# All experts' rows added to the residual on TensorE by one-hot products, gate and up in blocks of 32 slots, and another order of the experts

## The chip, the cores and the metric

One NeuronCore of a Trainium2 chip runs the whole kernel in one launch. The metric is the device time of one execution in microseconds; the median of three runs counts. The engines named below are PE (TensorE, matrix products and transposes), PEld (its weight loads, which go beside the products), DVE (VectorE), ACT (ScalarE), POOL (GpSimd) and SP (SyncE, which here issues the big DMAs).

## What is computed

Two transformer blocks over 512 tokens of width 1024, all in float32. The second block ends in a mixture of 32 experts, and only that part is touched by the change. Cut to what matters:

```python
def hier_moe(h, w_rg, b_rg, w_re, b_re, w_gate, w_up, w_down):
    # every token picks one group, and two experts in it, with weights top_w
    ...
    # expert e, for the rows x of the tokens that chose it:
    y = (silu(x @ w_gate[e]) * (x @ w_up[e])) @ w_down[e]
    # each row is scaled by its weight and added to its token
    ...

x = x + hier_moe(rmsnorm_2(x, norm2_g), ...)
```

`w_gate[e]` and `w_up[e]` are 1024 x 512, `w_down[e]` is 512 x 1024: 6 MB an expert, 192 MB in all. 512 tokens with two experts each make 1024 rows. For the given inputs the rows of experts 0 to 31 are 37, 57, 10, 30, 27, 23, 34, 20, 37, 16, 26, 2, 21, 11, 16, 15, 26, 40, 42, 48, 11, 31, 11, 31, 48, 36, 10, 81, 25, 85, 78, 39. Thirteen experts have over 32 rows, three of them (27, 29, 30) over 64.

## The kernel before

Everything up to the router takes about 1,140 us and is the same in both kernels, but for one small thing named below. Then the experts run one after the other, in the order 31, 30, ... 0.

**Weights.** `fetch` issues them from SP's queue in units of 2 MB, each two DMAs of 1 MB: two units of an expert hold halves of gate and up together, and one holds down. A ring of 9 units (three experts) is filled ahead; from then on a unit is fetched when PE has done with the one in its place, and SP's queue takes them in the order of a list, `plan`: the two gate/up units of expert i, then the down unit of expert i - 1.

**Rows.** An expert's rows sit in slots, 64 to a block. POOL gathers a block with an indirect DMA. A row of 1024 is kept as two halves in partitions 0 to 63 and 64 to 127 (`xs`; `xb` for a second block).

**PE's work for one expert** is: two transposes of the activations of the expert before (`at`), four of the next expert's rows (`xt`), gate and up (`gu_half`, once for each half), and down of the expert before (`expert_down`, name `yy`). The array's 128 columns are used as two tiles of 64 columns, side by side: one tile for the output columns of c = 0 and one for c = 1. A float32 product of 512 columns stands in the trace as two PE instructions, so that a half of gate/up and a whole down are each 16 instructions.

**More than 64 rows.** `tc.If(cnt > SLOTS)` runs a second block of 64 slots (`gv`, then `yv` after the down). There are two such branches per expert; all engines have them.

**The way back.** `expert_y` scales the rows of `yy` by their weights on ACT, and POOL scatters them by an indirect DMA to a buffer in DRAM, `y_d`, where each token has two places. (`clear_y` has set that buffer to zero in the first block's MLP.) When all is scattered, `add_y` reads `y_d` back, 4 MB, and adds it to the residual `x2` on DVE and POOL. The last two experts (DIRECT = 2) don't go that way: `add_direct` multiplies a one-hot matrix (which slot belongs to which token, `owned`) by their rows on PE, 64 slots of a half in each half of the array's rows, and DVE adds the product to `x2`.

Of the kernel before, what the change touches and what calls it, by code (L numbers as in the profile page):

```python
# [9 lines left out]
F32 = mybir.dt.float32  # L10
# [10 lines left out]
P = 128  # L21
# [67 lines left out]
def tile_kernel(tc, I, out, dbg=None, stop=None):  # L89
# [1135 lines left out]
    DIRECT = 2  # L1225
# [74 lines left out]
    loads = []  # L1300

    def fetch(srcs):
# [5 lines left out]
        for i, src in enumerate(srcs):  # L1308
            loads.append(nc.sync.dma_start(raw[:, i * 2048:(i + 1) * 2048], src))
# [6 lines left out]
    def src_d(e):  # L1316
        return [wd_d[e].rearrange("(h p j) d -> h p (j d)", h=2, j=2)[h] for h in range(2)]


    seq = list(range(NE))[::-1]  # L1320
    plan = []
    for i in range(NE + 1):
        if i < NE:
            plan += [src_gu(seq[i], 0), src_gu(seq[i], 1)]
        if i:
            plan.append(src_d(seq[i - 1]))
# [137 lines left out]
    gi_, si_, wsl, tkf = [], [], [], []  # L1464
    tps_ = bank("t")
    for blk in range(2):
# [9 lines left out]
        tkf.append(tki)  # L1476
        si_.append(by_halves(f"si{blk}", orf)[0])
        wsl.append(slot_weights(rtp, tps_[:, (2 + blk) * NE:(3 + blk) * NE], oh, f"m{blk}"))
    tail_.__exit__(None, None, None)
# [11 lines left out]
    y_h = y_d.rearrange("s (h d) -> (s h) d", h=2)  # L1491
# [7 lines left out]
    def scatter(ys, idx, dst=y_h):  # L1499
# [17 lines left out]
    def gu_half(ps, xT, W, h):  # L1517
# [8 lines left out]
    def expert_act(ps, blk=""):  # L1526
        a_ = mp.tile([P, 256], F32, tag=f"act{blk}", bufs=1 if blk else 2, name=f"act{blk}{uid()}")
        nc.scalar.activation(a_, ps[:, 0:256], AF.Silu)  # L1528
        nc.vector.tensor_tensor(a_, a_, ps[:, 256:512], op=ALU.mult)  # L1529
        return a_  # L1530

    def expert_aT(a_, blk=""):
        tp = tr_bank("at")
        av = a_.rearrange("s (p j) -> s j p", j=2)
        for j in range(2):
            nc.tensor.transpose(tp[:, j * P:(j + 1) * P], av[:, j, :], ident)
        aT = mp.tile([P, 2, P], F32, tag=f"aT{blk}", bufs=1 if blk else 2, name=f"aT{blk}{uid()}")
        nc.scalar.activation(aT.rearrange("p j s -> p (j s)"), tp[:, 0:256], AF.Copy)  # L1538
        return aT
# [220 lines left out]
```

## Time and profile before

| | |
|---|---|
| median of three runs | 1661.91 us (1661.04 to 1663.17) |
| the profiled execution | 1661.64 us, its span 1659.9 us |
| PE busy | 1529.6 us, 92% of the span |
| PEld busy | 1059.6 us, 64% |
| DVE busy | 710.4 us, 43% |
| ACT busy | 532.3 us, 32% |
| POOL busy | 184.7 us, 11% |
| SP's DMA queue | 317.12 MB, 51.2% of the span of 16 engines |

The span is the stretch that the profiler recorded, and the device time is 1.74 us longer. The shares are means over stages that are bound by different things: the experts are the last 520 us, in which DVE has little to do.

### The profile page before, as it was taken

What the parts mean: (1) busy time and instruction counts of PE and PEld (TensorE: products, weight loads), DVE (VectorE), ACT (ScalarE), POOL (GpSimd) and SP (SyncE); (2) the same over time, 40 slices, a digit from 0 to 9 for tenths busy, and PEclk for the clock granted to TensorE, in tenths of its full rate; (3) what the DMA queues carried; (4) which work ended last, traced back from release to release, by engine and by line L of the source; (5) the groups of instructions that cost most, each with busy time, mean ns of one, the idle gap of its engine ahead of it and who ended that gap; (6) DMA issues with size and microseconds to landing.
All of it is one profiled execution on the core that took longest, in us unless ns stands there. A gap on an engine that the chain in (4) does not pass through costs nothing. (4 is left out here: it accounts for less than half of the span.)

```text
span 1659.9 us, 20583 instructions
## 1 busy us (share of the span) xinstructions
PE 1529.6 (92%) x7494; PEld 1059.6 (64%) x7494; DVE 710.4 (43%) x1562; ACT 532.3 (32%) x1033; POOL 184.7 (11%) x199
## 2 busy tenths in 40 slices
PE   7999999899999999899999999987999988788776
PEld 7887776688888888688888777774333333233332
DVE  7699636663335444646874545543000100000003
ACT  6444437643324343443455433220111110010010
POOL 1000001220000000140000000012122221211112
PEclk9999999999999999999999999997999999999998
DMA  5313105025233323234222326646899999999995
GB/s 174 115 52 94 38 22 178 26 66 202 89 101 115 103 88 102 90 115 130 77 66 70 121 96 241 212 173 266 351 374 410 414 415 417 416 416 416 417 418 241
DMA packets 99327, 328.90 MB, mean 198 GB/s; under 512 B 17474, under 2 KB 26258, under 8 KB 74114
## 3 DMA queue, kind: packets, MB, share of 16 engines
q1 hardware_dynamic: 90866, 317.12, 51.2%
q0 software_dynamic: 8336, 10.14, 1.7%
q8 instruction: 75, 1.23, 0.3%
q14 instruction: 50, 0.41, 0.1%
HBM read 321.27 MB, written 24.92 MB: 209 GB/s over the span
## 5 line engine op out<-in xcount | busy, mean ns | idle before, releaser
L127 PE MATMUL mm<-wh,Ah 128*128 128x512 f32 (+3 forms) x800 | 307.4, 384 | 6.6 <-DVE gate L1211 2.1
L1522 PE MATMUL gu<-mr,xT 128*64 128x512 f32 x1024 | 251.6, 630 | 55.8 <-DMA mr<-in_w_expert_up_dram 51.3
L128 PE MATMUL mm<-wl,Ah 128*128 128x512 f32 (+3 forms) x800 | 299.1, 374 | 0.7 <-DVE wl L134 0.7
L129 PE MATMUL mm<-wh,Al 128*128 128x512 f32 (+3 forms) x800 | 299.5, 375 | 0.0
L134 DVE TENSOR_TENSOR wl<-raw,wh 128x1024 fp32r<-128x1024 f32 (+3 forms) x160 | 185.0, 1163 | 117.6 <-ACT wh L133 114.3
L133 ACT ACTIVATE wh<-raw 128x1024 fp32r<-128x1024 f32 (+3 forms) x164 | 164.1, 1008 | 146.0 <-PE mm L128 117.4
L1522 PEld LDWEIGHTS gu<-mr,xT 128*64 128x64 f32 x1024 | 81.8, 144 | 201.9 <-issue 198.8
L127 PEld LDWEIGHTS mm<-wh,Ah 128*128 128x128 f32 x800 | 152.3, 190 | 33.3 <-issue 4.9
L127 PE MATMUL mm<-Ah,wh 128*128 128x512 f32 x416 | 169.4, 407 | 0.0
L129 PEld LDWEIGHTS mm<-wh,Al 128*128 128x128 f32 x800 | 151.9, 190 | 25.8 <-DVE Al L134 0.7
L128 PEld LDWEIGHTS mm<-wl,Ah 128*128 128x128 f32 x800 | 152.5, 191 | 23.8 <-DVE wl L134 1.2
L129 PE MATMUL mm<-Ah,wl 128*128 128x512 f32 x416 | 163.2, 392 | 0.0
L128 PE MATMUL mm<-Al,wh 128*128 128x512 f32 x416 | 163.2, 392 | 0.0
L253 POOL TENSOR_TENSOR rr<-rm,mhalf 128x1 f32<-128x1 f32 (+3 forms) x40 | 32.5, 815 | 991.4 <-DVE rm L252 991.3
L1529 DVE TENSOR_TENSOR act<-act,gu 128x256 f32<-128x256 f32 x32 | 13.5, 421 | 281.6 <-ACT act L1528 281.6
L1546 PE MATMUL yy<-mr,aT 128*64 128x512 f32 x512 | 117.3, 594 | 1.7 <-ACT aT L1538 0.9
L1528 ACT ACTIVATE act<-gu 128x256 f32<-128x256 f32 x32 | 12.3, 384 | 274.3 <-PE gu L1522 274.3
L128 PEld LDWEIGHTS mm<-Al,wh 128*128 128x128 f32 x416 | 78.3, 188 | 17.6 <-issue 2.9
L127 PEld LDWEIGHTS mm<-Ah,wh 128*128 128x128 f32 x416 | 78.3, 188 | 17.2 <-issue 2.9
L129 PEld LDWEIGHTS mm<-Ah,wl 128*128 128x128 f32 x416 | 78.3, 188 | 15.9
L1546 PEld LDWEIGHTS yy<-mr,aT 128*64 128x64 f32 x512 | 40.9, 137 | 70.8 <-issue 56.9
L1514 DVE COPY xT<-xt 128x512 f32<-128x512 f32 x35 | 24.2, 691 | 143.3 <-PE xt L1512 143.3
(379 smaller groups left out, 1921.6 us busy)
## 6 DMA issues: line engine op xcount, KB each, us to landing
mr<-in_w_expert_gate_dram SPq DMA_DIRECT2D x64, 1024.0 KB
mr<-in_w_expert_up_dram SPq DMA_DIRECT2D x64, 1024.0 KB
mr<-in_w_expert_down_dram SPq DMA_DIRECT2D x64, 1024.0 KB
raw<-in_w_in_dram SPq DMA_DIRECT2D x56, 512.0 KB
raw<-in_w_up_dram SPq DMA_DIRECT2D x32, 512.0 KB
raw<-in_w_down_dram SPq DMA_DIRECT2D x32, 512.0 KB
raw<-in_w_out_dram SPq DMA_DIRECT2D x16, 512.0 KB
y_d<-zero SPq DMA_DIRECT2D x4, 1024.0 KB
```

The source lines that it names most:

```text
L127: nc.tensor.matmul(ps, ah, bh, start=first, stop=False)
L128: nc.tensor.matmul(ps, ah, bl, start=False, stop=False)
L129: nc.tensor.matmul(ps, al, bh, start=False, stop=last)
L133: nc.scalar.activation(hi, src, AF.Copy)
L134: return lo_eng.tensor_tensor(lo, src, hi.bitcast(F32), op=ALU.subtract)
L253: nc.gpsimd.tensor_tensor(r[:, :n], m[:, :n], mhalf[:, :n], op=ALU.pow)
L1514: nc.vector.tensor_copy(xT.rearrange("p j s -> p (j s)"), tp)
L1522: nc.tensor.matmul(ps[c * 64:(c + 1) * 64, :].rearrange("s (w f) -> s w f", w=2), xT[:, j, h * 64:(h + 1) * 64], wv[:, :, j, c * 256:(c + ...
L1528: nc.scalar.activation(a_, ps[:, 0:256], AF.Silu)
L1529: nc.vector.tensor_tensor(a_, a_, ps[:, 256:512], op=ALU.mult)
L1546: nc.tensor.matmul(ps[c * 64:(c + 1) * 64, :], aT[:, j, h * 64:(h + 1) * 64], wv[:, h, j, c * 512:(c + 1) * 512], start=h + j == 0, stop=h ...
```

## The change

- Nothing is scattered, and `y_d` is not cleared. For every expert the rows of `yy`, scaled, are split into a high part `yh` (ACT) and a rest `yl` (DVE), both float32r, and a one-hot matrix is made with a comparison on DVE (`own`). `add_y` is now a generator that does a token tile of 128 at each step: four products (two parts, two halves of the row) into two PSUM banks (`dr`, a pool of two banks of its own), then two DVE adds of 128 x 512 to `x2`. An expert's four steps are handed out two places later in the loop, between its successors' products.
- Gate and up work in blocks of 32 slots: four tiles of 32 columns side by side, 256 output columns each. The first block always runs. The second (`gv`) runs under `If cnt > 32`, once for each half of the rows. More than 64 rows run under a third If as before in blocks of 64 (`gw`, `yv`). With the one behind the down there are four branches per expert.
- The order of experts is 16 to 31, then 0 to 15. Eleven of the thirteen experts with over 32 rows are among the first 18 in this order, all three with over 64 among the first 15. The order before had those three at places 2, 3 and 5.
- `yy`'s pool has one bank instead of two, the transposes' two instead of three. The down weights lie in SBUF in another order, which cuts their DMAs in pieces of 4 KB instead of 8 KB. At the end of `plan` the down unit of the expert before the last comes ahead of the last expert's gate/up units.

```diff
-        if c == 4:
-            with tc.issue_after(wload[0].ins):
-                clear_y(up)
...
     def src_d(e):
-        return [wd_d[e].rearrange("(h p j) d -> h p (j d)", h=2, j=2)[h] for h in range(2)]
-
-
-    seq = list(range(NE))[::-1]
+        return [wd_d[e].rearrange("(h c p) d -> h p c d", h=2, c=2)[h] for h in range(2)]
+
+
+    seq = [(e + NE // 2) % NE for e in range(NE)]
...
+        gu_ = [src_gu(seq[i], 0), src_gu(seq[i], 1)] if i < NE else []
+        dn_ = [src_d(seq[i - 1])] if i else []
+        plan += dn_ + gu_ if i == NE - 1 else gu_ + dn_
...
+    io512 = rt("io512", [S])
+    for t in range(NT):
+        nc.vector.tensor_scalar(io512[:, t * P:(t + 1) * P], iota, float(t * P), None, op0=ALU.add)
...
-    yy_ps = ps_moe.enter_context(tc.tile_pool(name="yy_ps", bufs=2, space=PSUM))
+    yy_ps = ps_moe.enter_context(tc.tile_pool(name="yy_ps", bufs=1, space=PSUM))
     b1_ps = ps_moe.enter_context(tc.tile_pool(name="b1_ps", bufs=1, space=PSUM))
-    tr_ps = ps_moe.enter_context(tc.tile_pool(name="tr_ps", bufs=3, space=PSUM))
+    tr_ps = ps_moe.enter_context(tc.tile_pool(name="tr_ps", bufs=2, space=PSUM))
+    dr_ps = ps_moe.enter_context(tc.tile_pool(name="dr_ps", bufs=2, space=PSUM))
...
-    def gu_half(ps, xT, W, h):
+    def gu_half(ps, xT, W, h, q, between=None):
+
+        wv = W.rearrange("p (w j f) -> p w j f", w=2, j=4)
+        for j in range(4):
+            for c in range(4):
+                nc.tensor.matmul(ps[c * 32:(c + 1) * 32, 0:256].rearrange("s (w f) -> s w f", w=2),
+                                 xT[:, j, h * 64 + q * 32:h * 64 + (q + 1) * 32], wv[:, :, j, c * P:(c + 1) * P],
+                                 start=h == 0 and j == 0, stop=h == 1 and j == 3)
+            if between and j % 2:
+                next(between, None)
+
...
+    def expert_aT(acts):
+
         tp = tr_bank("at")
...
+        for q in range(2):
+            nc.tensor.transpose(tp[:, q * P:(q + 1) * P], acts[q], ident)
+        aT = mp.tile([P, 4, 64], F32, tag="aT", bufs=1, name=f"aT{uid()}")
+        nc.scalar.activation(aT.rearrange("p k (q s) -> p k q s", q=2),
+                             tp[:, 0:256].rearrange("p (q k s) -> p k q s", q=2, k=4), AF.Copy)
         return aT
...
+        wv = W.rearrange("p (k d) -> p k d", k=4)
+        for k in range(4):
+            for c in range(2):
+                nc.tensor.matmul(ps[c * 64:(c + 1) * 64, :], aT[:, k, :], wv[:, k, c * 512:(c + 1) * 512],
+                                 start=k == 0, stop=k == 3)
+
+    owned = mp.tile([P, 2, S], F32R, tag="ohp", bufs=1, name="owned")
+
+    def expert_y(e, ps, blk):
+
+        own = owned[:, blk, :]
+        nc.vector.tensor_scalar(own, io512, tok[blk][:, e:e + 1], None, op0=ALU.is_equal)
+        w_ = wsl[blk][:, e:e + 1]
+        yh = mp.tile([P, 512], F32R, tag="yh", bufs=2, name=f"yh{uid()}")
+        yl = mp.tile([P, 512], F32R, tag="yl", bufs=2, name=f"yl{uid()}")
+        split(yh, yl, ps, scale=w_)
+        return own, yh, yl
+
+    def add_y(y_, last=False):
+
+        own, yh, yl = y_
         for t in range(NT):
...
+            pss = [dr_ps.tile([P, 512], F32, tag="dr", name=f"dr{uid()}") for _ in range(2)]
+            for k, part in enumerate((yh, yl)):
+                for h in range(2):
+                    hs = slice(h * 64, (h + 1) * 64)
+                    nc.tensor.matmul(pss[h], own[hs, t * P:(t + 1) * P], part[hs, :], start=k == 0, stop=k == 1)
             for h in range(2):
-                hs = slice(h * 64, (h + 1) * 64)
-                nc.tensor.matmul(pss[h], own[i][hs, t * P:(t + 1) * P], direct[i][hs, :],
-                                 start=i == 0, stop=i == DIRECT - 1)
-        for h in range(2):
-            cl = slice(h * 512, (h + 1) * 512)
-            nc.vector.tensor_tensor(x2[:, t, cl], x2[:, t, cl], pss[h], op=ALU.add)
-        nc.sync.dma_start(out[0, t * P:(t + 1) * P, :], x2[:, t, :])
+                cl = slice(h * 512, (h + 1) * 512)
+                nc.vector.tensor_tensor(x2[:, t, cl], x2[:, t, cl], pss[h], op=ALU.add)
+            if last:
+                nc.sync.dma_start(out[0, t * P:(t + 1) * P, :], x2[:, t, :])
+            yield
...
+    def down(j):
+
+        W = unit()
+        ps = yy_ps.tile([P, 512], F32, tag="yy", name=f"yy{j}")
+        expert_down(ps, aT, W)
+        ys[j] = expert_y(seq[j], ps, 0)
+        with tc.If(cnt[j] > SLOTS):
+            aT1 = expert_aT64(act1[j % 2])
+            ps1 = b1_ps.tile([P, 512], F32, tag="b1", name=f"yv{j}")
+            expert_down(ps1, aT1, W)
+            run(add_y(expert_y(seq[j], ps1, 1)))
...
+        if i >= NE - 1:
+            run(add_y(ys.pop(i - 2)))
+            aT = expert_aT(acts[(i - 1) % 2])
+            down(i - 1)
+        if i == NE:
+            break
+        e = seq[i]
+        cnt[i] = nc.values_load(cnti[0:1, e:e + 1], min_val=0, max_val=S)
+        adds = add_y(ys.pop(i - 2)) if 1 < i < NE - 1 else iter(())
+        W = [unit()]
+        a_ = acts[i % 2]
+        ps = gu_ps.tile([P, 512], F32, tag="gu", name=f"gu{e}")
+        gu_half(ps, xT, W[0], 0, 0, adds)
+        ps1 = b1_ps.tile([P, 512], F32, tag="b1", name=f"gv{e}")
+        with tc.If(cnt[i] > 32):
+            gu_half(ps1, xT, W[0], 0, 1)
+        if 0 < i < NE - 1:
+            aT = expert_aT(acts[(i - 1) % 2])
+        x0 = xT
...
+        W.append(unit())
+        gu_half(ps, x0, W[1], 1, 0, adds)
+        expert_act(a_[0], ps)
+        with tc.If(cnt[i] > 32):
+            gu_half(ps1, x0, W[1], 1, 1)
+            expert_act(a_[1], ps1)
+        with tc.If(cnt[i] > SLOTS):
+            x1 = expert_x(x1b[i % 2], "1")
+            ps2 = b1_ps.tile([P, 512], F32, tag="b1", name=f"gw{e}")
+            for h in range(2):
+                gu_half64(ps2, x1, W[h], h)
+            expert_act(act1[i % 2], ps2)
+        if i + 2 < NE:
+            gather(x1b[i % 2], gi_[1][:, seq[i + 2]:seq[i + 2] + 1])
+        if 0 < i < NE - 1:
+            down(i - 1)
+    run(add_y(ys.pop(NE - 1), last=True))
```

**PE, an expert in the second half of the list, before.** `at`, `xt`, `gu` and `yy` are named above; `gv` and `yv` lie between a branch and the jump behind it. An x8 of products is 16 instructions.

```order
L1536 MATMUL at_13059<-ident,act_12962 128x128 x2
L1512 MATMUL xt_13064<-ident,xs_9753 128x128 x4
L1522 MATMUL gu_13050<-mr_13047,xT_12946 64x512 x8
L1608 TENSOR_LOAD cnti
L1624 COMPARE_AND_BRANCH
L1512 MATMUL xt_13090<-ident,xb_9749 128x128 x4
L1522 MATMUL gv_13097<-mr_13047,xT_13095 64x512 x8
L1522 MATMUL gv_13097<-mr_13074,xT_13095 64x512 x8
L1624 UNCONDITIONAL_BRANCH x2
L1522 MATMUL gu_13050<-mr_13074,xT_12946 64x512 x8
L1546 MATMUL yy_13122<-mr_13119,aT_13062 64x512 x8
L1638 COMPARE_AND_BRANCH
```

**PE, an expert at about the same place, after.** First the stretch behind the down of the expert before, up to the branch for the second block:

```order
L1544 MATMUL at_16121<-ident,act_9784 128x128
L1587 MATMUL dr_16079<-yh_15997,owned 128x512
L1587 MATMUL dr_16080<-yh_15997,owned 128x512
L1544 MATMUL at_16121<-ident,act_9785 128x128
L1510 MATMUL xt_16126<-ident,xs_9756 128x128 x2
L1587 MATMUL dr_16079<-yl_15998,owned 128x512
L1587 MATMUL dr_16080<-yl_15998,owned 128x512
L1510 MATMUL xt_16126<-ident,xs_9756 128x128 x2
L1587 MATMUL dr_16095<-yh_15997,owned 128x512
L1587 MATMUL dr_16095<-yl_15998,owned 128x512
L1587 MATMUL dr_16096<-yh_15997,owned 128x512
L1587 MATMUL dr_16096<-yl_15998,owned 128x512
```

and then, after four more products of this kind (the third token tile), from the branch on:

```order
L1635 TENSOR_LOAD cnti
L1642 COMPARE_AND_BRANCH
L1520 MATMUL gv_16103<-mr_16067,xT_15893 32x256 x16
L1642 UNCONDITIONAL_BRANCH x2
L1520 MATMUL gu_16070<-mr_16067,xT_15893 32x256 x16
L1587 MATMUL dr_16163<-yh_15997,owned 128x512
L1587 MATMUL dr_16164<-yh_15997,owned 128x512
L1587 MATMUL dr_16163<-yl_15998,owned 128x512
L1587 MATMUL dr_16164<-yl_15998,owned 128x512
L1654 COMPARE_AND_BRANCH
L1520 MATMUL gv_16103<-mr_16136,xT_15893 32x256 x16
L1654 UNCONDITIONAL_BRANCH x2
```

The transposes are now split up by products of the expert two places before (`dr`), three of whose four token tiles stand ahead of the first gate/up block, and the fourth between the two; one straight row of products became three branches and pieces of four shapes.

**DVE, the same stretch, after.** The adds of the four token tiles (L1590), the copy of the transposed rows (`xT`) and the one-hot matrix:

```order
L1590 TENSOR_TENSOR x_8768<-x_8768,dr_16552 128x512
L1590 TENSOR_TENSOR x_8768<-x_8768,dr_16553 128x512
L1590 TENSOR_TENSOR x_8768<-x_8768,dr_16568 128x512
L1590 TENSOR_TENSOR x_8768<-x_8768,dr_16569 128x512
L1512 COPY xT_16604<-xt_16599 128x512
L1635 TENSOR_LOAD cnti
L1642 COMPARE_AND_BRANCH
L1642 UNCONDITIONAL_BRANCH x2
L1590 TENSOR_TENSOR x_8768<-x_8768,dr_16617 128x512
L1590 TENSOR_TENSOR x_8768<-x_8768,dr_16618 128x512
L1590 TENSOR_TENSOR x_8768<-x_8768,dr_16633 128x512
L1590 TENSOR_TENSOR x_8768<-x_8768,dr_16634 128x512
```

Two adds stand for each token tile, in the order in which PE needs the two banks back. Before, DVE had a copy and a multiplication here.

## Rows read from the trace of the kernel before

**Rows 1.** Busy time in stretches of 50 us, while the experts run.

```profile
core 0: us, PE busy (x) PEld busy (x) DVE busy (x) ACT busy (x) POOL busy (x), PEclk, DMA share, GB/s
...
1250.00:1300.00 50.00, 48.32 (x228) 18.63 (x226) 4.45 (x8) 5.72 (x12) 12.82 (x13) 1.00 1.01 411
...
1500.00:1550.00 50.00, 38.44 (x171) 14.63 (x169) 3.34 (x6) 4.37 (x9) 9.20 (x9) 0.97 1.02 416
```

**Rows 2.** SP's queue: start, duration and tile of the weights' issues.

```profile
1157.81 0.34 SPq L1309 DMA_DIRECT2D mr<-in_w_expert_gate_dram  x1
...
1265.26 0.87 SPq L1309 DMA_DIRECT2D mr<-in_w_expert_down_dram  x2
...
1277.35 0.87 SPq L1309 DMA_DIRECT2D mr<-in_w_expert_down_dram  x2
...
1560.02 3.06 SPq L1309 DMA_DIRECT2D mr<-in_w_expert_down_dram  x2
...
1575.74 3.10 SPq L1309 DMA_DIRECT2D mr<-in_w_expert_down_dram  x2
```

**Rows 3.** PE's timeline, one expert and the start of the next.

```profile
1266.18 3.65 PE L1522 MATMUL gu<-mr,xT 128*64 128x512 f32 x16
1270.14 3.65 PE L1522 MATMUL gu<-mr,xT 128*64 128x512 f32 x16 [0.31 <-PEq L1624]
1273.60 3.63 PE L1546 MATMUL yy<-mr,aT 128*64 128x512 f32 x16
1277.38 0.47 PE L1536 MATMUL at<-ident,act 128*128 128x128 f32 x2
1277.69 0.65 PE L1512 MATMUL xt<-ident,xs 128*128 128x128 f32 x4
1278.27 3.65 PE L1522 MATMUL gu<-mr,xT 128*64 128x512 f32 x16
```

**Rows 4.** Groups by line from 1140 us to the end: busy time, mean ns of one.

```profile
L1546 PE MATMUL yy<-mr,aT 128*64 128x512 f32 x512 | 117.3, 594 | 1.7 <-ACT aT L1538 0.9 <-DMA mr<-in_w_expert_down_dram 0.6
...
L1587 DVE TENSOR_TENSOR x<-x,dr 128x512 f32<-128x512 f32 x8 | 5.2, 686 | 0.5
```

**Rows 5.** PE's timeline at the end of the second block's merge: float32r.

```profile
1051.37 0.40 PE L129 MATMUL mm<-ymh,wl 128*128 128x512 f32 x1
1051.60 0.39 PE L127 MATMUL mm<-ymh,wh 128*128 128x512 f32 x1
```

**Rows 6.** The timeline at the last expert's down: weight loads alone.

```profile
1633.25 0.20 PEld L1546 LDWEIGHTS yy<-mr,aT 128*64 128x64 f32 x4 [0.94 <-ACT aT L1538]
```

**Rows 7.** The timeline where `add_direct` runs: PE and DVE.

```profile
1637.06 5.66 PE L1583 MATMUL dr<-ys,owned 64*128 64x512 f32 x20 [0.16 <-PEq L1638]
...
1643.25 1.29 DVE L1587 TENSOR_TENSOR x<-x,dr 128x512 f32<-128x512 f32 x2
1643.99 2.58 PE L1583 MATMUL dr<-ys,owned 64*128 64x512 f32 x8 [1.26 <-DVE x L1587]
```

**Rows 8.** PE's timeline, first expert, and around two second blocks.

```profile
1142.82 14.85 PE L1522 MATMUL gu<-mr,xT 128*64 128x512 f32 x64
...
1177.23 0.64 PE L1512 MATMUL xt<-ident,xb 128*128 128x128 f32 x4
...
1185.77 0.63 PE L1512 MATMUL xt<-ident,xs 128*128 128x128 f32 x3
...
1196.77 0.51 PE L1536 MATMUL at<-ident,act 128*128 128x128 f32 x2
...
1201.30 1.02 PE L1522 MATMUL gu<-mr,xT 128*64 128x512 f32 x2
```

**Rows 9.** The chain that ended last, its end.

```profile
1624.85 11.88 DMA yt<-y_d
...
1651.02 0.65 DVE x L1587
```

**Rows 10.** Busy time where `clear_y` writes its zeros (columns as in 1).

```profile
390.00:400.00 10.00, 10.00 (x46) 8.29 (x45) 4.97 (x5) 3.41 (x5) 0.00 (x0) 1.00 0.82 279
```

More of the change, by code (lines that the diff above doesn't have):

```diff
@@ L1308, in fetch @@
         for i, src in enumerate(srcs):
-            loads.append(nc.sync.dma_start(raw[:, i * 2048:(i + 1) * 2048], src))
+            dst = raw[:, i * 2048:(i + 1) * 2048]
+            nc.sync.dma_start(dst if len(src.shape) == 2 else dst.rearrange("p (c d) -> p c d", c=2), src)
         return raw
@@ L1524, in gu_half, with expert_act @@
                                  start=h == 0 and j == 0, stop=h == 1 and j == 3)
[L1526 to L1532, printed above, removed]
-        tp = tr_bank("at")
[L1534 to L1538, printed above, removed]
+    def expert_act(a_, ps):
+        n = a_.shape[-1]
+        nc.scalar.activation(a_, ps[:, 0:n], AF.Silu)
+        nc.vector.tensor_tensor(a_, a_, ps[:, n:2 * n], op=ALU.mult)
@@ new lines, in expert_aT, with expert_aT64 @@
+    def expert_aT(acts):
+        tp = tr_bank("at")
+        for q in range(2):
[3 more added lines that the diff above has]
+                             tp[:, 0:256].rearrange("p (q k s) -> p k q s", q=2, k=4), AF.Copy)
+        return aT
+    def expert_aT64(a_):
+        tp = tr_bank("at")
+        for b in range(2):
+            nc.tensor.transpose(tp[:, b * P:(b + 1) * P], a_[:, b * P:(b + 1) * P], ident)
+        aT = mp.tile([P, 4, 64], F32, tag="aT1", bufs=1, name=f"aT1{uid()}")
+        nc.scalar.activation(aT.rearrange("p (c b) s -> p b c s", b=2),
+                             tp[:, 0:256].rearrange("p (b c s) -> p b c s", b=2, c=2), AF.Copy)
@@ L1539, in expert_aT @@
         return aT
     def expert_down(ps, aT, W):
-        wv = W.rearrange("p (h j d) -> p h j d", h=2, j=2)
-        for h in range(2):
-            for j in range(2):
-                for c in range(2):
-                    nc.tensor.matmul(ps[c * 64:(c + 1) * 64, :], aT[:, j, h * 64:(h + 1) * 64],
-                                     wv[:, h, j, c * 512:(c + 1) * 512], start=h + j == 0, stop=h + j == 2)
-    direct, own = [], []
-    def owners(e):
-        o = owned[:, len(own) * S:(len(own) + 1) * S]
-        tf = small.tile([P, 1], F32, tag="ss", name=f"tkf{e}")
-        nc.vector.tensor_copy(tf, tkf[0][:, e:e + 1])
-        for t in range(NT):
-            nc.vector.tensor_scalar(o[:, t * P:(t + 1) * P], iota, float(t * P), tf, op0=ALU.add, op1=ALU.is_equal)
-        own.append(o)
@@ L1560, in expert_y @@
-    def expert_y(e, ps, blk, to_y_d):
-        ys = mp.tile([P, 512], F32, tag="ys", bufs=4, name=f"ys{uid()}")
-        nc.scalar.activation(ys, ps, AF.Copy, scale=wsl[blk][:, e:e + 1])
-        if to_y_d:
-            scatter(ys, si_[blk][:, e:e + 1])
-        else:
-            direct.append(ys)
-    def add_y(t):
-        yt = rawp.tile([P, 4096], F32, tag="near", bufs=NEAR, name=f"yt{uid()}")[:, 0:2048]
-        with tc.issue_after(loads[-1].ins):
-            nc.sync.dma_start(yt, y_d[2 * t * P:2 * (t + 1) * P, :].rearrange("(p j) d -> p (j d)", j=2))
-        for cl, eng in ((slice(0, 640), nc.vector), (slice(640, D), nc.gpsimd)):
-            for k in range(2):
-                eng.tensor_tensor(x2[:, t, cl], x2[:, t, cl], yt[:, k * D:(k + 1) * D][:, cl], op=ALU.add)
@@ L1647, in tile_kernel @@
-    for t in range(NT):
-        add_y(t)
-    for t in range(NT):
-        add_direct(t)
+    acts = [[mp.tile([P, P], F32, name=f"act{q}{i}") for q in range(2)] for i in range(2)]
+    act1 = [mp.tile([P, 256], F32, name=f"actm{i}") for i in range(2)]
+    for a_ in acts:
+        nc.gpsimd.memset(a_[1], 0.0)
+    cnt, ys = {}, {}
+    def down(j):
[8 more added lines that the diff above has]
+            run(add_y(expert_y(seq[j], ps1, 1)))
```

67 lines of the change are left out of this document (9 added, 58 removed).

## The prediction

> **What bounds the kernel now.** I read three views. The first is the busy time in stretches of 50 us over the experts, to see whether PE or the weights' DMAs set the pace and when that changes. The second is SP's queue, since a fetch goes out when PE frees a unit and so shows the period of an expert. The third is PE's timeline, for what one expert costs there.
>
> In the stretch from 1250 us PE is busy for 48.3 of 50 us and the DMA engines are full too. From 1500 us PE is busy for 38.4 us, and the DMAs move 416 GB/s [rows 1]. SP's down issues are 12.09 us apart at 1265 to 1277 us, and 15.72 us apart at 1560 us [rows 2]. So PE eats up the three experts fetched ahead at about 12.1 us each, and then the DMAs' 15.7 us is the period until the weights are in. PE therefore has 3.6 us of slack per expert late in the list. The change has to fit into this.
>
> The 12.09 us can be taken apart by the starts on PE's timeline [rows 3]. A block of 16 instructions with nothing else between it and the next takes 3.46 us (1270.14 to 1273.60). The first half of gate/up takes 3.96, so the branch behind it, with the load of the count, costs 0.50. The down takes 3.78, so its branch with the change from tiles of 64 columns to the whole array costs 0.32. The six transposes and the change back take 0.89. Together: 3 x 3.46 + 0.50 + 0.32 + 0.89 = 12.06, the period but for rounding.
>
> **The change, part by part: an expert of up to 32 rows, on PE.**
>
> - Gate and up: half the columns per tile, and four tiles. The two tiles of now overlap fully: one instruction of this kind lasts 0.594 us [rows 4], a float32r one of as many columns lasts 0.39 and is followed by the next after 0.23 [rows 5], so 0.16 is the way through the array and 0.43 its own; 16 in 3.46 is 0.43 per pair. If four tiles do the same, a half takes 1.73 and both 3.46. Four weight loads of 64 columns pass in 0.20 us [rows 6], which just fits into the 0.22 that four products of 256 columns would take. I take 3.46. The far bound is 6.92, no gain at all.
> - Down stays at 3.46, transposes at 0.89.
> - Branches: four. One loads the count, 0.50, and three at 0.32 make 0.96: 1.46 together.
> - Changes of shape without a branch: the order after shows six more, between transposes, one-hot products, gate/up and down. The trace has no price of one by itself. It lies between nothing and 0.32 (branch and change together). I take the middle, 0.15, so 0.9.
> - One-hot products: 16 of 512 columns in float32r, at 0.23 us each one after the other [rows 5]. Two halves of the array's rows overlap, not always: 8 float32 instructions take 2.58 us [rows 7], where 8 x 0.43 and the way through would be 3.6 and pairs 1.9. A token tile's four take 0.46 side by side, 0.92 one after the other.
> - Waits for the two `dr` banks. A DVE add takes 0.686 us [rows 4], so two adds per token tile take 1.4 us, three times what the products take. The trace shows this wait: PE stood for 1.26 us until the first of two adds had gone by [rows 7]. Three tiles stand in a row. Tile 0 takes 0.46. Tiles 1 and 2 end after four adds, 2.74, the last products, 0.46, and some 0.2 through the pipeline, while two transposes (0.4) lie beneath. Tile 3 comes behind a gate/up block that hides its wait, 0.46. Sum: 0.46 + 3.4 - 0.4 + 0.46 = 3.9. The bounds are 1.84 (all side by side, no wait) and 5.5 (eight adds in the open).
>
> Sum for such an expert: 3.46 + 3.46 + 0.89 + 1.46 + 0.9 + 3.9 = 14.1 us, 2 more than before.
>
> The Trainium skill has a rule here, "TensorEngine Tiling (Array Packing)", Tiling Modes, that a change of tiling mode drains the engine. It speaks against the interleaving; the rows here only bound the price, and at 0.32 the sum would be 15.1 per expert.
>
> **Experts of more than 32 rows (13).** A second block costs 2 x 1.73 and two bodies behind branches, for which I take 0.25 each (between nothing and 0.50): 4.0 each.
>
> **Experts of more than 64 rows (3).** The old second block is still there: from its transposes to the next row behind it took 8.5 us for gate/up (1177.23 to 1185.77), and 4.5 for the down (1196.77 to 1201.30) [rows 8]. Behind it now come the split, 1.4, and eight adds with nothing to lie under, 5.5. Together 20 us each.
>
> **The sum.** 32 x 14.1 + 13 x 4.0 + 3 x 20 = 563 us, a mean of 17.6 us per expert. That is above the DMAs' 15.7, so PE sets the pace. The first gate/up starts at 1142.8 [rows 8]; nothing ahead of it changes that matters. The last expert's split and adds have nothing beneath them: about 5 us more than the sum holds. Last add: 1142.8 + 563 + 5 = 1711. Before, the last add ended at 1651.7 [rows 9], 8.2 us ahead of the span's end (the last store and the close), and this stays. The span is then 1719, and with the 1.74 us around the profiled span **1721 us**. The profiled execution took 1661.64, 0.3 below the median, so no correction. That is 3.6% slower.
>
> **What costs or gives nothing.** Clearing `y_d` lay beside a PE that was busy for 10.00 of 10 us [rows 10]. Without the scatter the DMAs carry about 0.13 MB less of some 6.5 MB per expert (1024 rows of 4 KB over 32): 0.3 us of 15.72, so 15.4. It lies under PE while PE sets the pace; were it not so, it would be worth 9 us. The read-back of 11.88 us and the adds behind it [rows 9] go, but they only become visible gain if the DMAs bound the end. Down weights in 4 KB pieces: even 5% on a third of the bytes is 0.3 us per expert, under the same cover. DVE gets 8 adds, the rest `yl`, the one-hot matrix and the copy, all below 8 us per expert: it does not become the bound as a whole, only at the banks. The order matters little: eleven of the thirteen dear experts come among the first 18, so PE falls behind early and stays behind, with the ring full.
>
> **Rivals.**
>
> *(a) PE keeps pace after all: faster.* If the adds slip under other work and a change of shape costs nothing, an expert costs 3.46 + 3.46 + 0.89 + 1.46 + 1.84 = 11.1. With 3.5 for each of 13 and 13 for each of 3 that is 440 us, 13.8 on average, less than the DMAs' 15.4. Then the weights set the end. The first fetch into the ring goes out at 1157.8 [rows 2], 29 experts follow at 15.4: 1604. Behind it lie the last down, the split and the adds, 10 us, and the same 9.9 as above: 1625 us, 2.2% faster. The point of decision is a mean of 15.75 us per expert on PE (1142.8 + 32 x 15.75 + 5 + 9.9 = 1662). For it: 1.9 us less per expert than I have, and the waits and changes are the terms with the widest bounds. Against it: the four branches and the three big experts stay whatever they do. Between 1625 and 1655 I give it 0.23.
>
> *(b) Four column tiles don't overlap fully: slower still.* If they gain three instead of four, each of the 90 half blocks (32 + 13 experts, two each) takes 2.31 instead of 1.73: 52 us more, 1773. For it: only two tiles are shown, and the weight loads have 10% to spare at best. Against: the two of now lose nothing [rows 3]. Chance 0.14. With no gain beyond two it would be 156 more, 1877, which I give 0.03.
>
> The Trainium skill, "TensorE: Matmul & The Clock Gate", part 3 (packing small matmuls), measures a gain of 3.07 for four tiles and 2.38 for three column tiles. By 3.07 the time would be about 1768; the two tiles of this trace gain the full 2, and no row here shows three or four.
>
> *(c) The two effects cancel*, within 0.2% of 1661.9 (which is about what a measurement of this kernel can tell from no change): 0.04.
>
> **How the numbers follow.** My sum as it stands has 0.56, with a range of its own of 1685 to 1755 (1 us per expert on either side). With (a) at 0.23, (b) at 0.17 and (c) at 0.04, faster has 0.23, same 0.04, slower 0.73. A range that leaves out the better half of (a) and most of (b) beyond 1778 goes from 1640 to 1778.
>
> **What would show it.** The down issues on SP should come 14 to 15 us apart for small experts and about 18 for those over 32, with PE busy and the DMAs' share below 1 over the whole list. The waits of PE should have the one-hot products waiting for DVE's adds, about 1.5 to 2 us per expert. A gate/up half should show 32 instructions in about 1.9 us; 2.4 or more speaks for (b). The last add should end near 1711 us. If instead the DMA share stands at 1.02 from about 1350 us on and PE waits for weights, (a) is right, and the term that I took too high is that of the waits or of the changes of shape. The prediction is wrong too if a third block's adds or a branch stop other engines for longer than the rows of before show.

## The result: 10.4% slower

The changed kernel took 1834.76 us (median of four runs, 1828.50 to 1846.04), the kernel before 1662.54 us in the same comparison. The ratio is 1.104, with a 95% interval of 1.099 to 1.109. The direction was forecast; the size was not: 1721 us were named, with 1640 to 1778 as the range.

The profiled execution is the longest of the four, 1846.04 us with a span of 1844.3. In stretches of 50 us, with the columns of [rows 1]:

```profile
core 0: us, PE busy (x) PEld busy (x) DVE busy (x) ACT busy (x) POOL busy (x), PEclk, DMA share, GB/s
1150.00:1200.00 50.00, 45.74 (x466) 21.69 (x455) 16.85 (x30) 4.53 (x13) 6.99 (x7) 1.00 0.92 366
...
1250.00:1300.00 50.00, 43.02 (x320) 20.00 (x312) 17.18 (x30) 4.32 (x10) 4.96 (x6) 0.83 0.83 331
...
1700.00:1750.00 50.00, 42.26 (x258) 19.90 (x257) 19.74 (x32) 3.50 (x8) 4.04 (x4) 0.73 0.87 344
```

PE is busy for 42 to 46 us of 50, and the weights' DMAs don't set the pace (their share stays below 1). New is the third number from the end: the granted clock of TensorE, which was 1.00 in [rows 1] while PE set the pace, is 0.83 and 0.73 in the second and third row. From 1150 to 1800 us its mean is 0.82.

SP's queue, which answers to [rows 2]:

```profile
1164.03 1.30 SPq L1305 DMA_DIRECT2D mr<-in_w_expert_down_dram  x2
...
1182.41 1.14 SPq L1305 DMA_DIRECT2D mr<-in_w_expert_down_dram  x2
...
1640.53 1.14 SPq L1305 DMA_DIRECT2D mr<-in_w_expert_down_dram  x2
...
1658.87 1.49 SPq L1305 DMA_DIRECT2D mr<-in_w_expert_down_dram  x2
...
1681.36 1.30 SPq L1305 DMA_DIRECT2D mr<-in_w_expert_down_dram  x2
```

A small expert takes 18.34 us (1640.53 to 1658.87) where 14.1 were forecast, and one with over 32 rows 22.5 (1658.87 to 1681.36) where 18.1 were. But early in the list an expert with over 32 rows took 18.4 (1164.03 to 1182.41), at the clock of 1.00 of the first row above. PE's timeline for that small expert, which answers to [rows 3]:

```profile
1640.55 0.30 PE L1544 MATMUL at<-ident,act 128*128 128x128 f32 x1 [0.16 <-PEq L1621]
1642.17 0.50 PE L1587 MATMUL dr<-yh,owned 64*128 64x512 f32 x2 [1.31 <-DVEq L1621]
1642.60 0.33 PE L1544 MATMUL at<-ident,act 128*128 128x128 f32 x1
1642.77 0.40 PE L1510 MATMUL xt<-ident,xs 128*128 128x128 f32 x2
1643.10 0.50 PE L1587 MATMUL dr<-yl,owned 64*128 64x512 f32 x2
...
1644.38 0.69 PE L1587 MATMUL dr<-yh,owned 64*128 64x512 f32 x1 [0.34 <-DVE x L1590]
...
1647.57 0.62 PE L1587 MATMUL dr<-yl,owned 64*128 64x512 f32 x1
1648.49 3.32 PE L1520 MATMUL gu<-mr,xT 128*32 128x256 f32 x32 [0.30 <-PEq L1642]
1651.74 0.50 PE L1587 MATMUL dr<-yh,owned 64*128 64x512 f32 x2
1652.08 0.39 PE L1587 MATMUL dr<-yl,owned 64*128 64x512 f32 x2
1653.22 1.93 PE L1520 MATMUL gu<-mr,xT 128*32 128x256 f32 x32 [0.75 <-PEq L1657]
1655.09 3.65 PE L1564 MATMUL yy<-mr,aT 128*64 128x512 f32 x16
1658.90 0.30 PE L1544 MATMUL at<-ident,act 128*128 128x128 f32 x1 [0.16 <-PEq L1621]
```

Two things are to be seen. Behind the down and one transpose, PE stands still for 1.31 us until the first one-hot product can run, and DVE's sequencer at L1621, the branch behind the down, is what it waits for. And the first gate/up half takes 3.25 us to the next start (1648.49 to 1651.74), the second, with the same 32 instructions, 1.87. The clock in stretches of 1 us says why; the first row is from after the stop:

```profile
1643.00:1644.00 1.00, 1.00 (x6) 0.50 (x4) 0.37 (x1) 0.38 (x1) 0.00 (x0) 1.00 0.94 393
1644.00:1645.00 1.00, 0.66 (x4) 0.43 (x3) 0.92 (x2) 0.00 (x0) 0.69 (x1) 0.76 0.99 418
1645.00:1646.00 1.00, 1.00 (x4) 0.47 (x2) 0.47 (x1) 0.00 (x0) 0.31 (x1) 0.50 1.02 418
1650.00:1651.00 1.00, 1.00 (x12) 0.46 (x8) 0.00 (x0) 0.00 (x0) 0.00 (x0) 0.50 1.03 414
1651.00:1652.00 1.00, 1.00 (x14) 0.49 (x8) 0.00 (x0) 0.00 (x0) 0.00 (x0) 0.82 0.57 217
1652.00:1653.00 1.00, 0.47 (x4) 0.03 (x2) 0.49 (x1) 0.00 (x0) 0.00 (x0) 1.00 0.09 37
```

The clock falls to 0.50 (1.2 GHz) in the stretch of one-hot products behind the stop, and comes back to 1.00 (2.4 GHz) some 7 us later, while gate/up runs without a gap. In stretches of 1 us the clock falls so 29 times between 1204 us and the end, about once per expert. Ahead of that the scheduler had laid the products among gate/up and transposes (the last two token tiles in the middle of the second half and behind it, 1174.88 and 1176.55), PE stood for 0.8 to 0.9 us shortly behind the down, and the clock stayed at 1.00. The next expert has the products laid alike, but a stop of 1.60 us ahead of them (1202.33), and there the clock falls for the first time. PE's waits, in total, times and longest:

```profile
PE dr L1587 <- DVEq L1621: 32.0, 24, 1.8
...
PE dr L1587 <- DVE x L1590: 14.6, 48, 0.8
```

### The profile page after: what moved, and what is told of

Read it like the earlier page. It is cut to its first block, busy times and chain, and to the rows that moved or that the text cites. A ratio compares the mean times of both kernels' runs of the same rounds, so it can differ in the third digit from the quotient of the medians.

```text
span 1844.3 us, 26395 instructions
## 1 busy us (share of the span) xinstructions
PE 1696.4 (92%) x9878; PEld 1170.4 (63%) x9878; DVE 912.0 (49%) x1903; ACT 532.5 (29%) x1046; POOL 138.1 (7%) x159
## 5 line engine op out<-in xcount | busy, mean ns | idle before, releaser
L1590 DVE TENSOR_TENSOR x<-x,dr 128x512 f32<-128x512 f32 x280 | 181.8, 684 | 209.5 <-PE dr L1587 206.4
L1520 PE MATMUL gu<-mr,xT 128*32 128x256 f32 x2048 | 161.4, 458 | 22.5 <-PEq L1657 15.4
L1587 PE MATMUL dr<-yh,owned 64*128 64x512 f32 x280 | 133.8, 628 | 52.4 <-DVEq L1621 32.0
L1520 PEld LDWEIGHTS gu<-mr,xT 128*32 128x32 f32 x2048 | 80.2, 130 | 102.9 <-issue 79.7
L1587 PEld LDWEIGHTS dr<-yh,owned 64*128 64x128 f32 x280 | 52.9, 228 | 128.1 <-DVE x L1590 59.9
L1587 PE MATMUL dr<-yl,owned 64*128 64x512 f32 x280 | 116.5, 539 | 0.9 <-DVE yl L136 0.9
## 6 DMA issues: line engine op xcount, KB each, us to landing
mr<-in_w_expert_down_dram SPq DMA_DIRECT2D x64, 1024.0 KB, 10.4
```

Source lines behind the costliest of these rows:

```text
L1520: nc.tensor.matmul(ps[c * 32:(c + 1) * 32, 0:256].rearrange("s (w f) -> s w f", w=2), xT[:, j, h * 64 + q * 32:h * 64 + (q + 1) * 32], wv[ ...
L1587: nc.tensor.matmul(pss[h], own[hs, t * P:(t + 1) * P], part[hs, :], start=k == 0, stop=k == 1)
L1590: nc.vector.tensor_tensor(x2[:, t, cl], x2[:, t, cl], pss[h], op=ALU.add)
```

## The experiments

Eleven kernels were run. A short name, as e1, is that of the run that begins with it. Times of different comparisons are set against the kernel before by their ratios; small experts' periods are gaps between SP's down issues.

### The stops taken away, the work kept: e1_spread

The first lines are those of the loop, the last those of `expert_down`:

```diff
-        gu_half(ps, xT, W[0], 0, 0, adds)
+        g0 = gu_half(ps, xT, W[0], 0, 0)
...
+        with tc.issue_after(g0.ins):
+            next(adds, None)
         gu_half(ps, x0, W[1], 1, 0, adds)
...
+            if between and k == 1:
+                with tc.issue_after(mm_.ins):
+                    next(between, None)
```

> The changed kernel, but the one-hot products of an expert come later: the first token tile behind the first gate/up half of the next expert but one, the second and third in the second half, the fourth in the middle of the next down. So the split has several us until its parts are read, and each pair of adds lies under other products; the work is the same. Theory A (the waits cost little by themselves, but PE stands still behind each down for the split and again for the two banks, and its clock falls to 1.2 GHz behind these stops): the granted clock is back at 0.97 or more from 1150 to 1600 us, PE needs 12 to 13 us per small expert, the weights set the end, 1625 to 1660 us. Rival B (narrow tiles and products on half the rows lower the clock by themselves, whatever PE waits for): the clock stays at 0.75 to 0.85, only the waits go, some 2 us per expert, 1765 to 1790 us.

Measured: 1726.07 us, ratio 1.038 (1.036 to 1.039). That is 109 us less than the changed kernel with the same instructions. Busy time in stretches of 100 us, columns as above:

```profile
1250.00:1350.00 100.00, 88.97 (x778) 38.97 (x774) 42.12 (x72) 9.62 (x22) 10.00 (x10) 0.97 1.02 411
1350.00:1450.00 100.00, 89.78 (x652) 40.19 (x650) 41.34 (x69) 7.58 (x18) 6.00 (x6) 0.90 0.57 220
...
1550.00:1650.00 100.00, 87.46 (x762) 38.61 (x758) 50.05 (x84) 9.72 (x22) 11.00 (x11) 0.98 1.02 411
```

The clock is 0.97 to 0.98 again where the three big experts are not. A small expert takes 13.5 us (1513.47 to 1526.99 to 1540.50). So theory A holds for the clock, and rival B falls: the same narrow tiles and half-row products run at full clock. The forecast of 1625 to 1660 us and of 12 to 13 per small expert was wrong all the same: the DMAs' share is 1.02 in two of the stretches and 0.57 in the one between, where the big experts are.

One expert's middle on PE shows the array's own prices:

```profile
1602.27 1.93 PE L1520 MATMUL gu<-mr,xT 128*32 128x256 f32 x32 [0.30 <-PEq L1647]
1604.13 0.50 PE L1592 MATMUL dr<-yh,owned 64*128 64x512 f32 x2
1604.47 0.39 PE L1592 MATMUL dr<-yl,owned 64*128 64x512 f32 x2
1605.84 1.07 PE L1520 MATMUL gu<-mr,xT 128*32 128x256 f32 x16 [0.97 <-DMA mr<-in_w_expert_down_dram]
1606.84 0.50 PE L1592 MATMUL dr<-yh,owned 64*128 64x512 f32 x2
1607.17 0.40 PE L1592 MATMUL dr<-yl,owned 64*128 64x512 f32 x2
1607.50 1.07 PE L1520 MATMUL gu<-mr,xT 128*32 128x256 f32 x16
```

32 instructions of gate/up on four tiles take 1.86 to the next start, and 16 take 1.00 (1605.84 to 1606.84), each time with a change of shape behind them. A token tile's four products take 0.66 (1606.84 to 1607.50). Between the halves, where two branches stand in a row, PE is idle for 0.97 us here (the row names a DMA, which came last by the profile) and for 0.74 in the two experts before 1540 us.

### The stop filled instead of taken away: e2_fill

```diff
+        if 1 < i < NE - 1:
+            fill = tr_bank("fill")
+            for _ in range(2):
+                nc.tensor.matmul(fill, ident, io512, start=True, stop=True)
```

> The changed kernel with two idle products added per expert (identity by a constant, 128 x 512, float32, some 1.7 us) right behind each down, where PE stands still for the split. The wait is filled, not taken away, and PE has more to do. Theory A: the clock is near 1.00 for most of an expert, and though work was added the kernel gets faster, 1710 to 1760 us. Rival B: the clock stays as it is, and the time too or a little longer, 1830 to 1850 us.

Measured: 1794.73 us, ratio 1.079 (1.077 to 1.082), 40 us less than the changed kernel though PE was given 1.7 us more to do per expert. The clock:

```profile
1550.00:1650.00 100.00, 89.83 (x727) 41.01 (x725) 40.28 (x71) 8.64 (x20) 12.12 (x12) 0.98 0.93 366
```

It is back at 0.94 to 1.00 in every stretch of 100 us from 1150 to 1750 us, and a small expert takes 16.3 us (1541.07 to 1557.34), though PE still waits 25.6 us in all for the banks. The gain was smaller than forecast. The run is not quite the one that was meant: with the added products the scheduler put two token tiles ahead of the first gate/up half and two behind it, where the change has three and one, so the 40 us are the filled stop and this together.

### The stop taken away, the waits for the banks left: e9_bunch

```diff
-        gu_half(ps, xT, W[0], 0, 0, adds)
+        g0 = gu_half(ps, xT, W[0], 0, 0)
...
-        gu_half(ps, x0, W[1], 1, 0, adds)
+        with tc.issue_after(g0.ins):
+            last_mm[0] = None
+            run(adds)
+        with tc.issue_after((last_mm[0] or g0).ins):
+            gu_half(ps, x0, W[1], 1, 0)
```

> The changed kernel, with all four token tiles of an expert's products in one row between the two gate/up halves of the next expert but one. The split has time, so PE doesn't stand behind the down, but the waits for the two banks all lie open: two adds for each of three tiles. Theory A1 (the long stop behind the down is what brings the clock down): granted clock 0.95 or more, some 15 to 16 us per small expert, 1740 to 1775 us. Theory A2 (the many short waits for the banks are enough): clock 0.88 or less, 1790 to 1830 us.

Measured: 1832.87 us, ratio 1.100 (1.095 to 1.104): no gain over the changed kernel, and a little above the range of A2. PE now waits in another place, and its clock is low there:

```profile
PE dr L1588 <- DVE x L1591: 35.3, 68, 0.9
```

```profile
1250.00:1350.00 100.00, 88.72 (x669) 40.04 (x667) 36.53 (x60) 7.29 (x17) 9.97 (x10) 0.82 0.78 307
...
1550.00:1650.00 100.00, 86.29 (x612) 37.69 (x614) 42.80 (x70) 7.01 (x16) 10.97 (x11) 0.87 0.90 347
```

The stop behind the down is gone but for 0.3 us (a wait for ACT, which e1 has too), and the clock is still 0.82 to 0.88 in every stretch of 100 us from 1250 to 1750 us. So A1, by which the long stop is needed, falls: a row of products with PE waiting for DVE between them, 68 times up to 0.9 us, does the same.

### The adds left out: e10_no_adds

```diff
-                nc.vector.tensor_tensor(x2[:, t, cl], x2[:, t, cl], pss[h], op=ALU.add)
+                if last:
+                    nc.vector.tensor_tensor(x2[:, t, cl], x2[:, t, cl], pss[h], op=ALU.add)
```

> The changed kernel without DVE's adds of the products to the residual, for all experts but the last; the products themselves stay (the output then lacks what these experts give). No wait for the banks is left, the stop behind the down stays. Theory A1: the clock stays low, 0.75 to 0.88, and only the waits of 1 to 2 us per expert go: 1770 to 1815 us. Theory A2: the clock is back at 0.95 or more, 14 to 15 us per small expert: 1725 to 1755 us.

Measured (two executions): 1703.47 us, ratio 1.024 (1.022 to 1.026), below both forecasts, a small expert at 13.5 us, the clock at 1.00 where the experts are small:

```profile
1250.00:1350.00 100.00, 90.83 (x806) 41.40 (x802) 15.63 (x29) 10.01 (x23) 10.97 (x11) 1.00 1.02 413
```

That looks like A2, but the run took away more than was meant. Behind the down PE now waits for 0.37 us, and for ACT:

```profile
1582.88 0.30 PE L1544 MATMUL at<-ident,act 128*128 128x128 f32 x1 [0.16 <-PEq L1622]
1583.56 0.50 PE L1587 MATMUL dr<-yh,owned 64*128 64x512 f32 x2 [0.37 <-ACTq L1622]
```

The changed kernel, the same place for the small expert that ends at 1658.87:

```profile
1658.84 0.69 ACT L135 ACTIVATE yh<-yy,wslm 128x512 fp32r<-128x512 f32 x1 [3.35 <-PEq L1621]
...
1659.56 0.75 DVE L136 SCALAR_TENSOR_TENSOR yl<-yy,wslm,yh 128x512 fp32r<-128x512 f32 x1 [3.75 <-ACTq L1621]
...
1660.52 0.50 PE L1587 MATMUL dr<-yh,owned 64*128 64x512 f32 x2 [1.31 <-DVEq L1621]
```

PE's product reads `yh`, which ACT has done at 1659.53, and the one-hot matrix, which DVE made before 1655 us, but it starts behind the end of `yl` (1660.31). In the changed kernel the last readers of the product's bank, in the order of the program, are the adds inside of the branch for more than 64 rows, behind the down. For a small expert they don't run, but PE's product has to wait until DVE has passed that branch, and in DVE's order the rest `yl` (0.75 us) stands ahead of it. Without the adds only the wait for ACT is left. So 0.37 of the 1.31 is ACT's part, and some 0.9 us comes of DVE at the branch; that this is the reason is read from the order and the releaser's name, no run changed it alone. For the clock this run says, with e1, that the kind of work doesn't lower it.

### Blocks of 64 with the products: e4_blocks64

```diff
-        gu_half(ps, xT, W[0], 0, 0, adds)
...
-        with tc.If(cnt[i] > 32):
-            gu_half(ps1, xT, W[0], 0, 1)
+        gu_half64(ps, xT, W[0], 0, adds)
```

> The other part alone: all rows by one-hot products as in the change, but gate and up in blocks of 64 slots with two tiles, and two branches per expert. Theory A: the stop behind the down stays, so the clock stays low, 0.75 to 0.88; gate/up of a small expert doubles, 3.5 to 5 us more per expert of up to 32 rows, and two branches less: 1850 to 1900 us. Rival C: the clock is back at 0.95 or more and this is faster than the changed kernel, 1740 to 1780 us.

Measured: 1863.34 us, ratio 1.121 (1.118 to 1.124), the clock 0.80 to 0.86 in every stretch of 100 us from 1250 us on. One of them:

```profile
1550.00:1650.00 100.00, 89.23 (x339) 35.82 (x336) 33.48 (x55) 7.27 (x15) 9.80 (x10) 0.84 0.78 299
```

So rival C, by which the narrow tiles are needed, falls; with this way back, the blocks of 32 with their two branches more are worth some 28 us.

### The scatter with the blocks of 32: e3_scatter_32

```diff
-        ys[j] = expert_y(seq[j], ps, 0)
+        expert_y(seq[j], ps, 0, j < NE - DIRECT)
...
-    run(add_y(ys.pop(NE - 1), last=True))
+    for t in range(NT):
+        add_y(t)
+    for t in range(NT):
+        add_direct(t)
```

The edit also brings back `clear_y`, the scatter and the read-back of the kernel before.

> One part of the change alone: gate and up in blocks of 32 slots, with the four branches, the new order and the new down layout, but the rows go back by the scatter and the read-back as before, the last two experts by one-hot products. Theory A: without stops behind the down the clock stays at 0.93 or more, PE needs some 9.5 us per small expert, the weights set the pace from the first refetch on, 1640 to 1655 us. Rival C (the tiles of 32 columns lower the clock): the clock is 0.75 to 0.85 while gate/up runs; the time may hide it behind the weights, 1645 to 1665 us.

Measured: 1659.46 us, ratio 0.998 (0.997 to 0.999). The DMAs' share is 0.98 to 1.02 from 1150 to 1550 us and PE waits 54 us for weights, so what the blocks of 32 save is not on the path. The clock of 0.92 to 1.00 in those 400 us again clears the narrow tiles:

```profile
1350.00:1450.00 100.00, 84.43 (x890) 41.03 (x892) 8.84 (x19) 11.97 (x29) 23.00 (x23) 1.00 1.02 411
```

The time came out above theory A's forecast and inside rival C's, but C's clock of 0.75 to 0.85 was not there.

### The order alone: e6_before_new_order and e5_old_order

```diff
-    seq = list(range(NE))[::-1]
+    seq = [(e + NE // 2) % NE for e in range(NE)]
```

This is the edit to the kernel before; e5_old_order is its reverse in the changed kernel.

> The kernel before with the new order alone. The weights set its pace in most of the list, and the big experts at places 12, 14 and 15 let the DMAs run ahead instead of holding up the first refetches. Theory: 1645 to 1656 us. Rival (the loss of time at the big experts is the same wherever they stand): 1660 to 1666 us. If the big experts in the middle leave the DMAs idle with a full ring: over 1668 us.

> The changed kernel with the order of experts of before (31 down to 0, those with over 64 rows at places 2, 3 and 5). As PE with its stops sets the pace nearly everywhere, the order should hardly matter: 1820 to 1845 us, clock still 0.75 to 0.85. If the order were a cause of the loss (the big experts in the middle of the list starve the weights' DMAs, which never catch up): 1790 us or less.

Measured: e6_before_new_order 1653.26 us, ratio 0.995 (0.993 to 0.996), the fastest kernel of this study, faster than both. e5_old_order (two executions) 1846.58 us, ratio 1.111 (1.108 to 1.113), a little above its forecast, against 1.104 with the new order: the order is no cause of the loss. The kernel before, in two stretches not shown yet, and under it the same two with the new order:

```profile
1150.00:1200.00 50.00, 46.52 (x210) 17.15 (x208) 4.69 (x9) 5.51 (x11) 7.09 (x7) 1.00 0.78 310
1200.00:1250.00 50.00, 47.26 (x214) 17.72 (x212) 4.36 (x8) 6.68 (x14) 10.69 (x11) 1.00 0.91 356
```

```profile
1150.00:1200.00 50.00, 48.07 (x212) 16.87 (x210) 4.45 (x8) 6.41 (x12) 12.15 (x12) 1.00 0.82 329
1200.00:1250.00 50.00, 44.03 (x204) 16.88 (x202) 4.45 (x8) 5.81 (x12) 12.23 (x12) 0.99 1.02 414
```

With the big experts later, the DMAs are full some 50 us earlier (0.82 and 1.02, against 0.78 and 0.91), and when the big experts come, PE is busy for 47 to 48 us of 50 and the DMAs are still full (1.01 to 1.02 from 1350 to 1450 us).

### Two branches less: e7_two_ifs and e8_two_ifs_old_order

On top of e1_spread, both halves of the second block behind one branch, and the block beyond 64 inside of it:

```diff
-        with tc.If(cnt[i] > 32):
-            gu_half(ps1, xT, W[0], 0, 1)
...
         with tc.If(cnt[i] > 32):
-            gu_half(ps1, x0, W[1], 1, 1)
+            for h in range(2):
+                gu_half(ps1, x0, W[h], h, 1)
             expert_act(a_[1], ps1)
-        with tc.If(cnt[i] > SLOTS):
+            with tc.If(cnt[i] > SLOTS):
```

> As the run with the products spread out, and with two branches less per small expert: the second block of 32 slots is done in one piece behind the first half of gate/up, under one If, and the block beyond 64 under an If inside of it. The run before gave 13.5 us per small expert on PE. Theory (branches at 0.5 to 1 us each are what is left over the array's own work): 12.0 to 12.5 us, the weights set the pace except around the three big experts, 1670 to 1695 us. Rival (the branches lie under the products' waits): no change, 1715 to 1730 us.

> The same with the order of experts of before. With PE below the weights' pace for small experts, the order counts: with the big ones early PE falls behind once, with a full ring, and the rest of the list makes it up. Theory: 15 to 35 us faster than with the new order, 1645 to 1670 us. Rival: no difference.

Measured: 1716.62 us, ratio 1.032 (1.030 to 1.034), and 1715.48 us, ratio 1.030 (1.028 to 1.033). A small expert takes 12.7 us on PE, so two branches are worth 0.8 us of it, but the whole gains only 9 us over e1_spread, and the order makes no difference; the total lies in the rival's range, though its reason is not the rival's. In e7_two_ifs:

```profile
1250.00:1350.00 100.00, 86.75 (x758) 36.23 (x757) 40.91 (x70) 8.53 (x20) 9.98 (x10) 0.95 1.01 411
1350.00:1450.00 100.00, 91.47 (x651) 40.40 (x651) 41.34 (x69) 7.57 (x18) 5.98 (x6) 0.88 0.56 214
```

Where the experts are small the DMAs are full, and PE stands still ahead of gate/up for up to 3.4 us (the view names the branch there; in e1 it names the weights, up to 3.3); around the three big ones (29 to 34 us from one down issue to the next) the ring is full and the DMAs stand half idle. Time lost in the one stretch is not won back in the other. Both forecasts were too low by this.

### The down weights in pieces of 4 KB: e11_4k

```diff
-        return [wd_d[e].rearrange("(h p j) d -> h p (j d)", h=2, j=2)[h] for h in range(2)]
+        return [wd_d[e].rearrange("(h c p) d -> h p c d", h=2, c=2)[h] for h in range(2)]
```

> The kernel before with the new order and the new layout of the down weights (DMA pieces of 4 KB instead of 8 KB), nothing else. The kernel before with the new order alone took 1653.3 us, and with blocks of 32 slots and this layout 1659.5. Theory (the smaller pieces cost the DMAs 1 to 2% of the down units, and the DMAs set the pace): 1656 to 1661 us. Rival (the pieces cost nothing, and the 6 us come from the blocks of 32 and their branches): 1651 to 1655 us.

The order is the new one here, and the transposes of the activations are changed to match.

Measured: 1657.57 us, ratio 0.997 (0.995 to 0.998), against 0.995 for the order alone; the time lies in the theory's range. The intervals overlap at their ends; the medians differ by 4.3 us, by the ratios 3.3. The traces say the same: from 1250 to 1600 us, where the DMAs' share is 1.01 to 1.02 in both, they move 412 to 415 GB/s here and 415 to 418 in e6_before_new_order, 0.7% less. So the smaller pieces cost the kernel before some 3 to 4 us, at the edge of what these runs can tell.

## Why the prediction was wrong

**What bounds the kernel** was right: PE sets the pace of the changed kernel, and the DMAs' share is below 1 in every stretch of 50 us.

**The step that failed is the one on waits, and with it the clock, which the working does not have at all.** The prediction put "waits for the two `dr` banks" at 3.9 us with the products, and has no term for the split in the sum of a small expert. In fact the products of an expert follow right behind its own down: PE stands for 1.31 us until DVE has passed the branch, 32.0 us in 24 waits. The banks cost less than was put: 14.6 us in all, some 0.5 per expert, where 2.1 of the 3.9 were waits. And every term was priced at the clock of 1.00 that the rows of before show [rows 1].

e1_spread, with the same instructions and the stops taken out, is 109 us faster than the change, about the whole of the miss (114 us). The profiled spans of the two lie 111.4 us apart, and the busy times tell where. The change, and under it e1_spread:

```profile
PE 1696.4 (92%) x9878; PEld 1170.4 (63%) x9878; DVE 912.0 (49%) x1903; ACT 532.5 (29%) x1046; POOL 138.1 (7%) x159
```

```profile
PE 1604.1 (93%) x9878; PEld 1124.2 (65%) x9878; DVE 913.6 (53%) x1903; ACT 532.5 (31%) x1046; POOL 138.1 (8%) x159
```

PE is busy 92.3 us longer with the same 9878 instructions, and idle only 19 us longer, since e1 has waits of its own in place of the stops (9.3 us for weights and 7.0 for ACT among them). So the standing itself is the smaller part of the loss, and slower work the greater. Gate/up in blocks of 32, in the same shapes, takes 29 us more (161.4 and 63.4 us against 142.2 and 53.3): that is the clock. The one-hot products take 59 us more (192.5 against 133.1), and there the order has a share that no run parts from the clock: in the change the parts of two token tiles come one by one, at full clock 1.25 us a tile (1429.97 to 1431.22), where pairs take 0.66; in e1 it is one tile. e2_fill, which has the clock but a longer way through each expert, is 40 us faster than the change. That e1's 1726 us lies beside the forecast of 1721 is luck: its small experts take less than 14.1, and the DMAs set the pace in parts of it.

**Why the clock falls** is shown as far as this: the tiles of 32 columns are neither needed for it (e4) nor enough (e3), the float32r products are not enough (e1, e10), and the stop behind the down is not needed (e9). What was enough to keep it is to lay the products apart (e1), or to fill the stop, with the order that this brought (e2). It falls where one-hot products in a row alternate with waits, and comes back in gate/up or down without a gap. But e2 still waits 25.6 us for the banks and mostly keeps its clock, and e9 waits 35.3 and doesn't. In e2 the token tiles stand two and two with a gate/up half between them, in e9 four in a row; whether that is the difference was not tried.

**The terms.** Four tiles side by side: right, and rival (b) is refuted. 64 gate/up instructions with nothing else between them take 3.48 at full clock (1183.21 to 1186.69 in the changed kernel), 1.74 for a half, where 1.73 was put; 16 on two tiles took 3.46 [rows 3], which is 6.92 for one tile alone if those two overlap fully, so the gain is the full four. The Trainium skill, "TensorE: Matmul & The Clock Gate", part 3, has 3.07 for four tiles, measured on row tiles; for the column tiles here these rows decide. One-hot products: four side by side were put at 0.46, and e1 shows 0.66, the term that was too low in itself. A change of shape: 0.15 was taken, and e1 shows 0.14 on the way into the products (16 instructions of gate/up and the change take 1.00, 32 and the change 1.86) and nothing on the way out, where the last pair takes 0.33 like the pair ahead of it. The Trainium skill's rule on it ("TensorEngine Tiling (Array Packing)", Tiling Modes), that a change of mode drains the engine, agrees with the 0.14, and the price is small. Branches: two in a row cost 0.8 to 1.0 from start to start in e1, not 0.64, and two less are worth 0.8 in e7. A small expert takes 13.5 in e1, where the terms of the prediction without their waits give 12.0; 0.3 of the difference is a wait for ACT behind the down, some 0.2 the branches, and most of the rest the products.

**What was to cost nothing.** The order: no clear difference in the change, as said, but worth 9 us in the kernel before, where the first stretch had DMAs to fill. The pieces of 4 KB: lost under PE in the change, which no run shows by itself; some 3 to 4 us where the DMAs set the pace (e11). The scatter's share: the DMAs' period of 15.4 without it was not seen; e8_two_ifs_old_order has 15.85 (1488.01 to 1630.66 in nine) where they set the pace, no less than the 15.72 of [rows 2], with the smaller pieces in it.

**Rival (a)**, that the kernel gets faster if PE's waits go, was wrong in its reckoning too. It set one sum for PE against one for the DMAs. e1 and e7 are bound by the DMAs at the small experts and by PE at the big ones, and the ring of three experts doesn't carry one over to the other, so that the greater of the two counts stretch by stretch.

**Why the change loses even with most of the clock back** (e7: 3.2%): it takes from the DMAs next to nothing of their 15.7 us per expert. On PE a small expert needs 13.5 us (12.7 in e7) instead of 12.1, though gate/up takes half the time, and a big expert's second block ends in 16 products with nothing beneath them (7.3 us in the changed kernel, 1387.70 to 1395.01). The kernel before had slack on PE for its big experts; this spends it.

## What to carry to other kernels

Before work is put on an engine that has slack, follow its first instruction back to everything it waits for: a buffer that was last read inside of a branch can mean a wait for the other engine to pass that branch, whether it is taken or not. Price new PE work at both levels of the clock when it comes in short pieces with waits between them, and look for a place between long dense products. And compare two bounds stretch by stretch, not by their sums.

## What was not expected of the hardware

PE's busy share did not tell of the clock: 42.3 busy us of 50 went with 0.73 in the change, and 38.4 of 50 with 0.97 in the kernel before [rows 1], where the idle time lay in a few waits for weights and the products in between were dense. Adding 1.7 us of useless products per expert, with the order that the scheduler then chose, made the kernel 40 us faster. And by the reading above, which no run tried alone, a wait for adds that didn't run, behind a branch on DVE, was the larger part (about 0.9 us) of a stop of 1.31.
